# Values held stationary in attention's sums over keys, a later residual scale and two experts summed by products

## The chip, the cores and the metric

The kernel runs on one core of a Trainium2 chip. Its time is the device time of one execution, in microseconds (us). Before the change it is 2874.34 us, the median of three runs (2862.95 to 2874.93). The engines are TensorE (PE; its weight loads are listed apart as PEld), VectorE (DVE), ScalarE (ACT), GpSimd (POOL) and SyncE (SP, which issues most DMAs). Each has a queue of its own and works it off in order.

## The reference

Two blocks of layers follow each other on 512 rows of width 1024, all in fp32. What the change touches is this:

```
P = softmax(mask(q k^T * scale + bias)) ;  o = P v        # per head, 64 wide, 128 queries at a time
  forgetting attention: 8 heads, causal                   (first block, stage ab)
  dilated attention:    8 heads, causal; sliding window with a sink: 8 heads   (stage cd)
  nsa: 16 heads; o = g0*o_compressed + g1*o_selected + g2*o_window             (second block)

h   = layer_norm(alpha*h + mix, ln_mix_g, ln_mix_b)
gate= top-2 of 16 experts per row, by groups of 4
ffn = sum_e gate[:, e] * (silu(h Wg_e) * (h Wu_e)) Wd_e
h   = layer_norm(alpha*h + ffn, ln_ffn_g, ln_ffn_b)       # twice, with gdn and with nsa as mix
```

512 keys are all that a query can select, so the selected branch of nsa is causal attention too, and so is its window.

## The kernel before

The program is written with a tile framework: tiles come from pools with a fixed number of buffers (three for P, three for the turned P, three for either half of a weight piece, two PSUM banks `lin`, one `pt`, three `s`, two `o`), and a scheduler sets the order of the instructions on every engine. Matrices are multiplied as high and low parts in fp32r: a weight piece of 128x1024 is copied from `ws` to `wh` on ACT (L130), and `wl = ws - wh` is made on DVE (L131). One such linear product is three matmuls (L151 to L153). The stages follow each other: ab with the forgetting attention, a cross attention, an MLP, cd with the dilated and the sliding attention, cross attention, MLP, then gdn, expert layer 0 (`out_moe`), nsa, expert layer 1.

**Attention.** `probs` multiplies queries with keys into a PSUM tile `s` (L296), DVE adds the bias strip and takes the minimum `mn` (L301, L302), and ACT writes P = exp and its row sum `den` (L304). `pv` turns P block by block on PE (L312), copies it out of PSUM (L781 on ACT or L783 on DVE in turn), and multiplies it with the values, P stationary and 64 columns of values moving, in plain fp32 (L316), which the trace shows as two records per matmul. Eight heads and query blocks share a PSUM tile; `o_norm` divides by `den` (L323), or in nsa `gated` multiplies with the gate over `den` and adds up the three branches (L1749, L1751 on DVE, L1753 on POOL); `pair_out` turns the result back (L332). The attention of nsa runs in eight chunks of two heads, each with a compressed branch (L1680 to L1703) and two causal ones.

**Expert layer.** `out_moe` finishes the mixer's output product into z, takes mean and variance of z, and keeps z in high and low parts `Rh`, `Rl`. `rescale` (L1204, L1205) then makes z the residual for the second LayerNorm, z*G + B, on POOL. `moe` finds the mask M of the chosen experts (L1310, a chain of small DVE operations), counts places with M on PE (L1342 to L1346), and loads the largest count for a branch on all engines (L1379, L1380): its body handles overfull experts and isn't entered here. Then, two experts at a time, one-hot matrices `oh` (L1508, DVE) gather rows of R by products (L1519), the expert's three matrices are applied, and its rows `ey` go to a table `yd` in DRAM. Each row of z is to get two experts' rows: POOL gathers the first of them from `yd` in four indirect DMAs (L1441) after expert 13, and DVE adds them (L1435); the second after the last expert, added by L1241 in `ln_out`. Only expert 15 is left out of the table and added by products with `oh` turned (L1232, L1233). `ln_out` does the second LayerNorm: square on ACT (L1243), a root by small DVE operations (L231 to L241), centring on ACT (L1246), times `ln_ffn_g` on POOL for three of four tiles (L1247), and the last step on DVE (L1258). R is what the next stage turns first (L1266).

## Time and profile before

| what | us |
|---|---|
| median of three runs | 2874.34 |
| profiled execution, its own time | 2872.59 |
| span of that execution in the trace | 2870.8 |
| PE, DVE, ACT, POOL busy | 2684.3, 1783.8, 1368.9, 231.1 |
| forgetting, dilated, sliding, nsa attention (stretches) | 118 to 205, 815 to 888, 888 to 995, 2287 to 2526 |
| expert layer 0: routing, loop, end | 1895 to 1930, 1930 to 2155, 2155 to 2190 |
| expert layer 1: routing, loop, end | 2575 to 2605, 2605 to 2835, 2835 to 2871 |

A stretch is a window of the span with the work of one stage; neighbours overlap, since the scheduler starts the next projections early. Busy time of an engine in a stretch against its length tells how near that engine is to being the limit there; idle time of the others costs nothing by itself. A wait is put down to the instruction that released it last.

### The profile page before, as it was taken

To read this page: it belongs to the slowest core of one execution; us is meant where nothing else is said; L and a number is where in the kernel's file an instruction comes from. 1 tells how busy PE (TensorE), PEld (TensorE's weight loads), DVE (VectorE), ACT (ScalarE), POOL (GpSimd) and SP (SyncE) were. 2 spreads that over 40 slices of the span, in tenths; PEclk is the share of its full clock that TensorE was granted. 3 is DMA by queue.
4 is the path that set the end of the run, shared out by engine and by line. 5 is a ranking of instruction groups with operands and counts; after the bars stand their busy time and mean duration, and the time that the engine had idled before them with its cause. 6 is when DMAs were issued, how large, how long until landed. Compare 5 with 4: busy or idle time off the path is not lost. (4 is left out here: it accounts for less than half of the span.)

```text
span 2870.8 us, 40089 instructions
## 1 busy us (share of the span) xinstructions
PE 2684.3 (94%) x15088; PEld 2290.8 (80%) x15088; DVE 1783.8 (62%) x3539; ACT 1368.9 (48%) x2545; POOL 231.1 (8%) x207
## 2 busy tenths in 40 slices
PE   8999999999999999999999999969986999986994
PEld 6888888888888988888887888967865888885873
DVE  6675564444457556545347777677766477677667
ACT  5654442333356434332246444327763355525774
POOL 1101010000111010000010000020001011011001
PEclk9999999999999999999999999979998999997998
DMA  4314133333233322335323222327885202013786
GB/s 134 98 56 137 60 107 96 96 95 99 86 88 85 125 78 63 104 100 176 99 93 120 69 69 80 103 65 244 263 282 181 66 23 74 16 49 128 260 264 218
DMA packets 123112, 333.65 MB, mean 116 GB/s; under 512 B 21781, under 2 KB 37813, under 8 KB 122905
## 3 DMA queue, kind: packets, MB, share of 16 engines
q1 hardware_dynamic: 120472, 322.48, 35.8%
q0 software_dynamic: 2432, 8.46, 0.8%
q8 instruction: 124, 2.03, 0.3%
q14 instruction: 84, 0.68, 0.1%
HBM read 301.49 MB, written 29.07 MB: 115 GB/s over the span
## 5 line engine op out<-in xcount | busy, mean ns | idle before, releaser
L130 ACT ACTIVATE wh<-ws 128x1024 fp32r<-128x1024 f32 (+2 forms) x521 | 534.1, 1030 | 888.5 <-PE lin L152 609.5
L131 DVE TENSOR_TENSOR wl<-ws,wh 128x1024 fp32r<-128x1024 f32 (+2 forms) x521 | 622.1, 1199 | 230.8 <-ACT wh L130 228.7
L151 PE MATMUL lin<-xs,wh 128*128 128x512 f32 (+2 forms) x1080 | 427.3, 396 | 7.7 <-ACT xs L196 6.3
L152 PE MATMUL lin<-xs,wh 128*128 128x512 f32 (+2 forms) x1080 | 427.7, 396 | 2.6 <-DVE xs L197 2.6
L153 PE MATMUL lin<-xs,wl 128*128 128x512 f32 (+2 forms) x1080 | 426.5, 395 | 0.9 <-DVE wl L131 0.9
L151 PEld LDWEIGHTS lin<-xs,wh 128*128 128x128 f32 (+2 forms) x1080 | 202.1, 187 | 51.0 <-ACT xs L196 7.2
L152 PEld LDWEIGHTS lin<-xs,wh 128*128 128x128 f32 (+2 forms) x1080 | 202.2, 187 | 47.2 <-DVE xs L197 6.9
L153 PEld LDWEIGHTS lin<-xs,wl 128*128 128x128 f32 (+2 forms) x1080 | 202.1, 187 | 42.1 <-DVE wl L131 1.4
L346 DVE TENSOR_TENSOR h<-lin,h 128x512 f32<-128x512 f32 x112 | 77.4, 691 | 247.7 <-PE lin L153 247.6
L151 PE MATMUL lin<-sr,wh 128*128 128x512 f32 x512 | 199.2, 389 | 0.0
L152 PE MATMUL lin<-sr,wh 128*128 128x512 f32 x512 | 199.2, 389 | 0.0
L153 PE MATMUL lin<-sr,wl 128*128 128x512 f32 x512 | 199.2, 389 | 0.0
L733 DVE SCALAR_TENSOR_TENSOR ra<-lin,bc 128x512 f32<-128x512 f32 x64 | 44.3, 692 | 166.8 <-PE lin L153 164.3
L1519 PE MATMUL o<-oh,Rh 128*128 128x256 f32 x512 | 133.5, 293 | 8.1 <-PEq L1380 4.9
L304 ACT ACTIVATE P<-s,mn 128x256 f32<-128x256 f32 (+1 forms) x224 | 114.2, 514 | 52.4 <-DVE mn L302 50.0
L1519 PE MATMUL o<-oh,Rl 128*128 128x256 f32 x512 | 132.1, 290 | 3.7 <-PEq L1380 3.7
L152 PE MATMUL s<-wl,exh 128*128 128x512 f32 x256 | 106.2, 415 | 12.7 <-DVE wl L131 12.6
L151 PE MATMUL s<-wh,exh 128*128 128x512 f32 x256 | 102.9, 405 | 12.3 <-ACT wh L130 12.1
L153 PEld LDWEIGHTS lin<-sr,wl 128*128 128x128 f32 x512 | 96.1, 188 | 20.1
L152 PEld LDWEIGHTS lin<-sr,wh 128*128 128x128 f32 x512 | 96.1, 188 | 19.9
L151 PEld LDWEIGHTS lin<-sr,wh 128*128 128x128 f32 x512 | 96.1, 188 | 19.8
L1519 PEld LDWEIGHTS o<-oh,Rh 128*128 128x128 f32 x512 | 101.3, 198 | 12.1 <-DVE oh L1508 7.0
(605 smaller groups left out, 6225.0 us busy)
## 6 DMA issues: line engine op xcount, KB each, us to landing
ws<-in_moe_wgu SPq DMA_DIRECT2D x128, 512.0 KB, 5.3
ws<-in_mlp_wu SPq DMA_DIRECT2D x64, 512.0 KB, 3.6
ws<-in_mlp_wd SPq DMA_DIRECT2D x64, 512.0 KB, 3.6
ws<-in_moe_wd SPq DMA_DIRECT2D x64, 512.0 KB, 5.2
yd<-ey SPq DMA_DIRECT2D x60, 256.0 KB, 3.3
ws<-in_gdn_w SPq DMA_DIRECT2D x24, 512.0 KB, 3.6
ws<-in_ab_w SPq DMA_DIRECT2D x16, 512.0 KB, 4.3
ws<-in_xa_wk SPq DMA_DIRECT2D x16, 512.0 KB, 3.8
```

The lines of the kernel that those rows point to most:

```text
L130: nc.scalar.activation(wh, ws, AF.Copy)
L131: nc.vector.tensor_tensor(wl, ws, rd(wh), op=OP.subtract)
L151: mm(out, a[0], b[0], start=start, stop=False)
L152: mm(out, a[0], b[1], start=False, stop=False)
L153: mm(out, a[1], b[0], start=False, stop=stop)
L304: nc.scalar.activation(P[:, :nk], p[:, :nk], AF.Exp, bias=mn, scale=-1.0, accum_out=den)
L346: self.nc.vector.tensor_tensor(self.hT[n], p, self.hT[n], op=OP.add)
L733: nc.vector.scalar_tensor_tensor(a, p, 0.0, rms()[1], op0=OP.max, op1=OP.mult)
L1519: nc.tensor.matmul(p[:, j * 256:(j + 1) * 256], Rs[t][i][:, f * 128:(f + 1) * 128], oh[:, t], start=t + i == 0, stop=t == NT - 1 and i == 1)
```

## The change

It has three parts.

1. *Attention.* Each P is divided by its row sum before it is turned (`weigh`: a reciprocal of 128x1 on DVE, L335, then a multiplication of P on POOL, with the gate of the branch in nsa). `turn` turns P as before, three PSUM tiles per causal head, and splits them in high and low parts (ACT one, DVE the other, L107 and L108). The values are kept as one fp32r tile with high and low part side by side, 128 columns per head, and are the stationary operand; the turned P moves, 128 to 256 columns at a time, and sums for all 512 queries gather in one PSUM tile per head (`causal`, twelve matmuls; eight for a sliding head). `head_out` adds its two halves, and nothing is turned back. In nsa the compressed branch gathers into the same tile, and the next chunk's is computed ahead. Two of three turned tiles of a head take buffers of the weight pieces. The sink of the sliding attention becomes one more column of the exponential. For room, the residual of ab and cd is dropped and loaded again (16 DMAs, after 8 writes in cd), and nsa's bias strips are loaded per chunk and not ahead of expert layer 0.
2. *Residual scale.* z*G + B is done by DVE in the expert loop, one tile after experts 5, 7, 9 and 11; two of the four split pairs of z and the first one-hot products are written in other places around the branch.
3. *Last two experts.* Experts 14 and 15 are both left out of the table and added by products; both gathers from DRAM follow expert 13; `ln_out` does its centring and gain in one DVE operation per tile and no longer on ACT and POOL.

The core of the diff:

```diff
+    def weigh(self, P, nk, den, gate=None):
+        r = self.small((128, 1), "rd")
+        self.nc.vector.reciprocal(r, den)
+        if gate is None:
+            self.nc.gpsimd.tensor_scalar(P[:, :nk], P[:, :nk], r, None, op0=OP.mult)
+        else:
+            self.nc.gpsimd.tensor_scalar(P[:, :nk], P[:, :nk], r, gate, op0=OP.mult, op1=OP.mult)
+
+    def turn(self, Ps, PT):
+        p, n = self.psum("o"), 0
+        for P, nb in Ps:
+            for b in range(nb):
+                self.nc.tensor.transpose(p[:, n * 128:(n + 1) * 128], P[:, b * 128:(b + 1) * 128], self.ident)
+                n += 1
+        self.split(p[:, :n * 128], *(x[:, :n * 128] for x in PT))
+
+    def turned(self):
+        self.uid += 1
+        return [self.wp.tile([128, 1024], F32R, tag=tag, name=f"PT{tag}_{self.uid}", bufs=BUFS[tag]) for tag in ("wh", "wl")]
+
+    def causal(self, o, P, V, first=True, last=True):
+        mm = self.nc.tensor.matmul
+        PT = self.turned()
+        for qb in (3, 2):
+            self.turn([(P(qb), qb + 1)], [x[:, (qb - 2) * 512:(qb - 1) * 512] for x in PT])
+        for k, i in ((0, 0), (1, 0), (1, 1), (3, 0), (3, 1), (2, 0), (2, 1), (0, 1)):
+            x = PT[i].rearrange("p (q c) -> p q c", q=2)[:, k // 3:, k * 128:(k + 1) * 128]
+            mm(o[:, 256 + k // 3 * 128:], V(k), x, start=first and k + i == 0, stop=False)
+        PT = [self.t("PT", F32R, "PT") for _ in range(2)]
+        p1 = P(1)
+        self.turn([(P(0), 1), (p1, 2)], PT)
+        for k, i in ((0, 0), (1, 0), (1, 1), (0, 1)):
+            mm(o[:, k * 128:256], V(k), PT[i][:, k * 256:256 + k * 128], start=False, stop=last and (k, i) == (0, 1))
+
+    def head_out(self, e, o, y):
+        u = self.t("oh")[:64]
+        self.nc.scalar.activation(u, o[64:], AF.Copy)
+        self.nc.vector.tensor_tensor(y[e * 64:e * 64 + 64], o[:64], u, op=OP.add)
...
-        def rescale(t):
-            nc.gpsimd.tensor_tensor(z[t], z[t], G, op=OP.mult)
-            nc.gpsimd.tensor_tensor(z[t], z[t], Bv, op=OP.add)
...
+    def rescale(self, x, gain):
+        for g, op in zip(gain, (OP.mult, OP.add)):
+            self.nc.vector.tensor_tensor(x, x, g, op=op)
...
-        for t in range(NT):
-            rescale(t)
-        space = self.all_space()
+        oh = self.one_hot(0, pos3, iota, "h")
+        begun = [self.gather(Rs, oh, r) for r in range(2)]
+        space = self.all_space("h")
         mx = nc.values_load(mxi[0:1, 0:1], min_val=0, max_val=S)
         with self.tc.If(mx > CAP):
...
         for i in range(0, 16, 2):
             h = [self.expert_up(layer, i + j, xT) for j in range(2)]
+            if i == 14:
+                break
             self.expert_down(layer, i, h[0], yd)
...
+            if i in (4, 6, 8, 10):
+                self.rescale(z[i // 2 - 2], gain)
             if i == 12:
                 ys = [self.collect(yd[:1 + 12 * CAP], idx[0], t) for t in range(NT)]
+                yg = [self.collect(yd[:1 + 14 * CAP], idx[1], t) for t in range(NT)]
...
-        y = self.expert_down(layer, 15, h[1], None)
-        yg = [self.collect(yd[:1 + 15 * CAP], idx[1], t) for t in range(NT)]
+        y = [self.expert_down(layer, 14 + e, h[e], None) for e in range(2)]
...
         def add(t):
-            nc.vector.scalar_tensor_tensor(z[t], yg[t], w[:, t:t + 1], z[t], op0=OP.mult, op1=OP.add, accum_out=m)
...
+            for c in range(2):
+                p, cs = self.psum("s" if (2 * t + c) % 5 < 3 else "o"), slice(c * S, (c + 1) * S)
+                for e in range(2):
+                    for i in range(2):
+                        nc.tensor.matmul(p, ohT[e][:, t * 128:(t + 1) * 128], y[e][i][:, cs], start=e + i == 0, stop=e + i == 2)
+                nc.vector.scalar_tensor_tensor(z[t][:, cs], p, w[:, t:t + 1], z[t][:, cs], op0=OP.mult, op1=OP.add,
+                                               accum_out=m[:, c:c + 1])
...
-            if t < NT - 1:
-                nc.scalar.activation(Rs[t], z[t], AF.Identity, bias=m)
-                nc.gpsimd.tensor_tensor(Rs[t], Rs[t], G, op=OP.mult)
-            else:
-                nc.vector.scalar_tensor_tensor(Rs[t], z[t], m, G, op0=OP.add, op1=OP.mult)
+            nc.vector.scalar_tensor_tensor(Rs[t], z[t], m, G, op0=OP.add, op1=OP.mult)
```

The order of POOL's queue at the routing of layer 0, up to the branch; z are the residual tiles (the last two of four are shown), the memsets belong to the body of the branch. Before:

```order
L1204 TENSOR_TENSOR z_15839<-z_15839,ln_mix_g_16125 128x1024
L1205 TENSOR_TENSOR z_15839<-z_15839,ln_mix_b_16127 128x1024
L1204 TENSOR_TENSOR z_15840<-z_15840,ln_mix_g_16125 128x1024
L1205 TENSOR_TENSOR z_15840<-z_15840,ln_mix_b_16127 128x1024
L1452 MEMSET ov_16624 128x2
L1452 MEMSET ov_16625 128x2
L1379 TENSOR_LOAD mxi_16590
L1380 COMPARE_AND_BRANCH
```

Now:

```order
L1554 MEMSET ovw_17198 128x2
L1554 MEMSET ov_17196 128x2
L1554 MEMSET ov_17197 128x2
L1467 TENSOR_LOAD mxi_17131
L1468 COMPARE_AND_BRANCH
```

All eight operations on z have left the queue.

DVE's queue of layer 0 around the gather that follows expert 13: `wl` are weight splits, `exl` and `ehs` an expert's inputs, `yg` the gathered rows. Before:

```order
L131 TENSOR_TENSOR wl_20431<-ws_20429,wh_20430 128x1024
L1435 SCALAR_TENSOR_TENSOR z_15837<-yg_20393,wl_18408,z_15837 128x512 x2
L131 TENSOR_TENSOR wl_20443<-ws_20441,wh_20442 128x1024
L131 TENSOR_TENSOR wl_20455<-ws_20453,wh_20454 128x1024
L131 TENSOR_TENSOR wl_20472<-ws_20470,wh_20471 128x1024
L1435 SCALAR_TENSOR_TENSOR z_15838<-yg_20397,wl_18408,z_15838 128x512
L131 TENSOR_TENSOR wl_20484<-ws_20482,wh_20483 128x1024
L1537 SCALAR_TENSOR_TENSOR eh_20465<-eh_20465,s_20416 128x256
L1435 SCALAR_TENSOR_TENSOR z_15838<-yg_20397,wl_18408,z_15838 128x512
```

Now:

```order
L108 TENSOR_TENSOR exl_20854<-ex_20894,exh_20853 128x512
L131 TENSOR_TENSOR wl_21006<-ws_21004,wh_21005 128x1024
L1510 SCALAR_TENSOR_TENSOR z_16378<-yg_20937,wl_18943,z_16378 128x512 x2
L1510 SCALAR_TENSOR_TENSOR z_16379<-yg_20941,wl_18943,z_16379 128x512 x2
L1510 SCALAR_TENSOR_TENSOR z_16380<-yg_20945,wl_18943,z_16380 128x512 x2
L1510 SCALAR_TENSOR_TENSOR z_16381<-yg_20949,wl_18943,z_16381 128x512 x2
L131 TENSOR_TENSOR wl_21018<-ws_21016,wh_21017 128x1024
L131 TENSOR_TENSOR wl_21030<-ws_21028,wh_21029 128x1024
L131 TENSOR_TENSOR wl_21047<-ws_21045,wh_21046 128x1024
```

The additions of the first gather stood singly or in twos between weight splits, and now stand eight in a row ahead of the next three.

DVE's queue inside a chunk of nsa: L302 takes the minimum of a tile `s` (its second row reads the result `mn`), ACT's exponential needs it, and `den` is the sum that ACT writes. Before:

```order
L301 TENSOR_REDUCE mf_22374<-s_22370 128x1
L1751 TENSOR_TENSOR acc_22148<-pt_22174,rg_22295 128x512
L302 ISA s_22370,mn_22348<-s_22370,strip_18301,mf_22374 128x256
L302 ISA mn_22348 128x1
L783 COPY PT_22364<-o_22359 128x512
L301 TENSOR_REDUCE mf_22393<-s_22389 128x1
L1751 TENSOR_TENSOR gtmp_22345<-pt_22340,rc_22169 128x512
L302 ISA s_22389,mn_22348<-s_22389,strip_18300,mf_22393 128x256
L302 ISA mn_22348 128x1
L301 TENSOR_REDUCE mf_22410<-s_22406 128x1
```

Now:

```order
L301 TENSOR_REDUCE mf_23784<-s_23780 128x1
L108 TENSOR_TENSOR PT_23723<-o_23746,PT_23722 128x384
L302 ISA s_23780,mn_23778<-s_23780,strip_23012,mf_23784 128x256
L302 ISA mn_23778 128x1
L335 RECIPROCAL rd_23788<-den_23779 128x1
L302 ISA s_23809,mn_23807<-s_23809,strip_23012 128x256
L302 ISA mn_23807 128x1
L108 TENSOR_TENSOR PTwl_23757<-o_23771,PTwh_23756 128x512
L335 RECIPROCAL rd_23815<-den_23808 128x1
```

The reciprocal of each `den` follows the minimum of the same tile, after no instruction or one.

## Rows read from the trace of the kernel before

**Rows 1.** The page: the span, and TensorE's busy time, share of the span and instructions.
```profile
span 2870.8 us, 40089 instructions
...
PE 2684.3 (94%) x15088; PEld 2290.8 (80%) x15088; DVE 1783.8 (62%) x3539; ACT 1368.9 (48%) x2545; POOL 231.1 (8%) x207
```

**Rows 2.** The table of stretches: length, busy time of each engine, granted clock, DMA.
```profile
core 0: us, PE busy (x) PEld busy (x) DVE busy (x) ACT busy (x) POOL busy (x), PEclk, DMA share, GB/s
118.00:205.00 87.00, 81.77 (x534) 71.09 (x533) 67.61 (x186) 57.99 (x138) 8.76 (x11) 1.00 0.13 41
815.00:888.00 73.00, 72.30 (x434) 61.83 (x433) 53.09 (x117) 48.34 (x108) 16.80 (x16) 1.00 0.30 81
888.00:995.00 107.00, 103.24 (x756) 96.12 (x755) 74.38 (x177) 61.29 (x154) 5.10 (x4) 0.95 0.38 116
2287.00:2526.00 239.00, 230.56 (x1650) 208.06 (x1649) 171.79 (x580) 131.49 (x372) 25.37 (x46) 0.98 0.11 36
1930.00:2155.00 225.00, 207.74 (x1103) 172.31 (x1102) 159.71 (x204) 165.62 (x251) 5.49 (x5) 0.98 0.80 263
```

**Rows 3.** What PE waited for, whole span: us in total, times, longest.
```profile
PE pt L1342 <- DVE M L1310: 33.7, 2, 17.5
```

**Rows 4.** Timelines of DVE and POOL before M: start, duration, engine, operation [idle, releaser].
```profile
1893.00 2.30 DVE L241 SCALAR_TENSOR_TENSOR b<-u,b 128x1 f32<-128x1 f32 x1
...
1904.14 0.16 DVE L241 SCALAR_TENSOR_TENSOR b<-u,b 128x1 f32<-128x1 f32 x1
...
1916.99 2.34 POOL L1205 TENSOR_TENSOR z<-z,ln_mix_b 128x1024 f32<-128x1024 f32 x1
...
1917.13 2.28 DVE L1310 TENSOR_TENSOR M<-e1e,e2e 128x64 fp32r<-128x64 f32 x1
...
2598.15 2.36 DVE L1310 TENSOR_TENSOR e2e<-e2e,e1e 128x64 f32<-128x64 f32 x1
```

**Rows 5.** Timelines of DVE, POOL and PE behind the last expert of both layers.
```profile
2168.03 1.29 DVE L1241 SCALAR_TENSOR_TENSOR z<-yg,wh,z 128x1024 f32<-128x1024 f32 x1 [2.17 <-DMA yg<-yd,ii]
...
2173.07 8.92 POOL L1247 TENSOR_TENSOR R<-R,ln_ffn_g 128x1024 f32<-128x1024 f32 x3 [6.90 <-ACT R L1246]
...
2173.25 3.25 DVE L131 TENSOR_TENSOR wl<-ws,wh 128x1024 fp32r<-128x1024 f32 x1
...
2185.63 1.12 PE L1266 MATMUL o<-c_ident,R 128*128 128x128 f32 x4 [22.28 <-DVE R L1258]
...
2851.04 1.82 DVE L237 SCALAR_TENSOR_TENSOR u<-b,h 128x1 f32<-128x1 f32 x1
```

**Rows 6.** Groups by line, nsa attention: count, busy us, mean ns, idle before, releasers.
```profile
L316 PE MATMUL pt<-vv,PT 128*128 128x64 f32 x640 | 88.5, 280 | 2.9 <-ACT PT L781 1.3 <-DVE PT L783 0.4
...
L304 ACT ACTIVATE P<-s,mn 128x512 f32<-128x512 f32 (+3 forms) x128 | 66.7, 525 | 34.7 <-DVE mn L302 32.8 <-PE o L312 1.4
...
L783 DVE COPY PT<-o 128x512 f32<-128x512 f32 (+1 forms) x64 | 31.4, 490 | 38.8 <-PE o L312 36.8 <-PE s L296 1.2
...
L304 ACT ACTIVATION_READ_ACCUMULATOR P<-s,mn 128x1 f32 x128 | 25.2, 197 | 0.0
...
L1749 DVE SCALAR_TENSOR_TENSOR acc<-pt,rg,acc 128x64 f32<-128x64 f32 x64 | 13.0, 278 | 2.0 <-PE pt L316 1.8 <-POOL ovx L1452 0.2
...
L131 DVE TENSOR_TENSOR wl<-ws,wh 128x1024 fp32r<-128x1024 f32 x10 | 12.2, 1222 | 0.6 <-ACT wh L130 0.5
...
L1753 POOL TENSOR_TENSOR acc<-acc,gtmp 128x512 f32<-128x512 f32 x8 | 10.2, 1277 | 117.0 <-DVE gtmp L1751 117.0
```

**Rows 7.** Timeline of PE: PV records, and products of 256 columns.
```profile
889.16 1.77 PE L316 MATMUL pt<-v,PT 128*128 128x64 f32 x14
...
2451.74 0.29 PE L151 MATMUL lin<-wh,ny 128*128 128x256 f32 x1
...
2451.86 0.28 PE L152 MATMUL lin<-wl,ny 128*128 128x256 f32 x1
```

**Rows 8.** What DVE waited for in the nsa attention.
```profile
DVE rg L1719 <- ACT P L304: 5.2, 10, 0.6
```

348 lines of the change are left out of this document (192 added, 156 removed).

## The prediction

> **What bounds the kernel now.** I read the page first: TensorE (PE) is busy for 2684.3 us of the span of 2870.8 [rows 1]. So time can come back in two kinds of place: where PE's own work shrinks, and where PE stands still. The table of stretches [rows 2] tells them apart. In the three attention stages of the first block (118 to 205, 815 to 888, 888 to 995 us) and in the nsa attention (2287 to 2526) PE is busy for 94 to 99% of the time, and VectorE (DVE) comes second with 70 to 78%. The list of PE's waits gives the largest hole: the routing mask M, 33.7 us in two waits, one per expert layer [rows 3]. The next one is R, the rows after the last LayerNorm of layer 0, 22.28 us [rows 5]. The change touches all of these.
>
> **Routing: POOL's rescale taken out.** Before M runs a chain of small DVE operations. One takes 0.16 us (1904.14), but six of layer 0 took some 2.2 us each, the first at 1893.00, the last, M, at 1917.13 [rows 4]. Each of the six lies under a multiplication or addition of 128x1024 on GpSimd (POOL): the one at 1916.99 takes 2.34 us, and M, started 0.14 us later, ends 0.08 us after it. These are the rescale of z, eight operations per layer. The change does them on DVE later. Six excesses of 2.0 us are 12; the order of DVE's queue up to M stays as it was, so I count 11.5 us in layer 0, and 11 in layer 1, where also six were stretched (the last at 2598.15, 2.36 us). The order holds five of the 32 gather products ahead of the branch, worth about 1 us a layer. **Sum 24 us, 20 to 26.**
>
> **The end of an expert layer.** PE's wait for R ends at 2185.63 [rows 5]. Inside it lie the second gather from DRAM, for which DVE still stood 2.17 us at 2168.03; four additions of 1.29 us after it; three POOL multiplications by the gain, 8.92 us from 2173.07; and two weight splits that these stretched, the first to 3.25 us, where one takes 1.22 [rows 6]. Now the last two experts come by products, nothing is gathered here, and DVE makes R. For the first R there is left a quarter of the additions, a square on ScalarE (ACT), a root, and two DVE operations of 1.29: about 9 us against 27 from the last expert product. But sixteen extra products of 512 columns (twice the 0.12 of 256 columns [rows 7], 3.8 us) come partly ahead of it, and the other three R follow at DVE's pace. I take 13 us for layer 0 (10 to 16). In layer 1 what goes is the stretch of three operations under the same POOL step (the first at 2851.04, 1.82 us; some 6 in all): 6 us (4 to 8). **Sum 19 us, 14 to 24.**
>
> **What the expert loop pays.** Eight DVE operations of 128x1024 per layer, at 1.22 us as a weight split [rows 6], are 9.8 us in a stretch of 225 in which DVE is busy for 160 and PE for 208 [rows 2]. They stand in DVE's queue ahead of weight splits for which PE waits next; and the additions of the first gather, so far singly between splits, now stand eight in a row (four tiles at 1.29, 5.2 us) behind the landing of the gather. Their cover is the weight tiles split ahead. If it holds, nothing is lost; if it fails, 9.8 and 5.2 a layer. I take 2.5, nearer to the free end, since DVE has 65 us to spare. **Loss 5 us, 0 to 30.**
>
> **Attention, PE's part.** Fourteen PV records of 64 columns take 1.77 us [rows 7], of which the last one's 0.28 [rows 6] overlaps nothing: 0.115 from start to start. nsa has 640 [rows 6], 74 us, and loses 64 products and 48 transposes besides, 12 us. It gets 32 causal heads of twelve products with at most 256 columns, 0.12 each [rows 7], 1.4 us a head, and 7 us of others: 52. PE saves 33 us there, by the same count 9 in each of the first two stages of the first block, and 7 in the third. PE in nsa would be at 198 of the present 239 us.
>
> **Attention, DVE's part.** In nsa DVE loses 64 copies of the turned P (31.4 us), 64 additions of 128x64 (13.0) [rows 6] and some 16 of gating. It gets, per head, three splits of 1280 columns in all, which today's four copies of 0.49 show as 1.8 us, together 58; 16 additions of two halves of 512 columns, half of 1.29 each, 10; and 128 reciprocals at 0.1 to 0.19, 13 to 24. So its work goes from 172 to about 200 us, level with PE. And there is a new wait. The reciprocal needs the sum of the exponentials, which ACT writes with the same P. The order has 50 of nsa's 128 reciprocals directly behind the read of their own minimum, and 39 with one instruction between. ACT needs 0.525 us for the mean exponential and 0.197 to read its sum [rows 6], overlapping by some 0.1. DVE has this wait already, once a branch after the smallest P: 5.2 us in ten times [rows 8]. For larger P it is 0.6 to 0.8. Going through the order and taking off the work that stands between, I get some 40 us of waiting in nsa and 5 in each other stage. 200 and 40 are 240: **the DVE queue needs about what the stage takes now**, and PE's 33 us turn into waits on DVE. Part of the 40 may be time in which DVE would be idle anyway (67 us today). I take a gain of 3 us for nsa, between a gain of 28 (the waits fall into idle time) and a loss of 20 (they come on top). In the first block, with the same terms: forgetting attention, DVE 68, 14 and 5 are 87 of 87 us, no gain; dilated, 53, 14 and 5 are 72 of 73, 2 us; sliding, 74, 10 and 5 are 89 of 107 with PE at 96, 6 us. **Sum 11 us, from a loss of 25 to a gain of 48.**
>
> **POOL's new step.** Each P is multiplied on POOL before it is turned. No row shows POOL with one input; the nearest is its addition of 128x512, 1.277 us [rows 6]. I take that for the largest P as the upper end and half of it as the lower. At the upper, which I use, POOL works about 100 of nsa's 239 us, and a P comes 1.3 us later, with three buffers for P and 1.9 us per P. By itself that bounds nothing.
>
> M and the POOL row above it [rows 4] show a lock. The Trainium skill, page "SBUF — State Buffer", section "Who interferes with whom", says that a DVE instruction with two SBUF inputs contends with a GpSimd instruction that reads SBUF, and that the second to issue blocks fully. By this rule the new step, which reads P from SBUF, would bring into the attention what leaves the routing, and the second rival's sum would hold in place of mine.
>
> **The sum.** 24 and 19 less 5 is 38 us for the expert layers, and 11 for the attention: 49. The profiled execution took 2872.6 us (a span of 2870.8 and 1.8 around it), 1.7 under the median of 2874.3. 2872.6 less 49 is 2823.6: **2824 us.**
>
> **Rivals.**
> - The reciprocals' waits fall into idle time of DVE. For it: 36.8 us of DVE's idle time in nsa lie before the copies of P [rows 6], waiting for transposes. Then PE's saving shows, 28 in nsa and 20 in the first block; with 38 that is 86, 2787 us.
> - POOL's step holds DVE, as the rescale did. There are 224 P; it decides the sign once a P costs the path 0.23 us more than I count, for 52 us eat up 38 and 14 (the bound below). For it: the weight splits, the splits of Q and K in the forgetting attention, and the rotations of the dilated heads read two SBUF tiles. Against: most DVE steps of a P read PSUM and one tile. If every P stops DVE for half of a POOL step of 0.8 us, 224 times 0.4 are 90 us: **2914 us, slower than before**.
> - The expert loop takes back the routing's gain: DVE's block of additions and the rescales hold up the weight splits, 30 us in place of 5: 2849 us.
> - The routing doesn't shorten, because something else ends there last: 24 us less, 2848. The rows of M and POOL speak against it.
>
> **How the numbers follow.** Forecast 0.53, first rival 0.21, second 0.08, third and fourth together 0.18. A measurement of this kernel can tell about 0.5%, 14 us, from no change. The forecast's own spread is 2803 to 2847. The range goes down to the first rival with a few us under it, and up over the third: 2782 to 2862. Faster by over 0.5% (under 2860) holds the forecast, the first rival and most of the third: 0.85. Within 0.5%: the rest of the third, 0.07. Slower: the second, 0.08.
>
> **What the changed profile would show.** M's two waits at 8 to 9 us each, and no small DVE operation of 2 us ahead of them; R's wait at 8 to 12 us; reciprocals waiting for ACT's P for some 40 us in nsa, PE's busy time there near 198 and the stage still near 236 us. I am wrong if nsa shrinks by 20 us or more (the waits were covered), if DVE operations with two SBUF inputs take 2 us in numbers in the attention (the lock), or if PE's waits for wl in the expert loop grow by more than 10 us.

## The result and the profile after

The changed kernel takes **3059.07 us**, the median of four runs (3049.82 to 3065.92), against 2874.64 us before (four runs, 2862.95 to 2879.53): a ratio of 1.0642, with a 95% interval of 1.0613 to 1.0671. It is 184 us slower where 50 us of gain were forecast, and the time lies 197 us above the upper end of the range. It is also beyond the one rival that ended slower (2914).

The page after, whose two rows answer to [rows 1]:

```profile
span 3060.6 us, 39865 instructions
...
PE 2779.6 (91%) x14584; PEld 2320.9 (76%) x14584; DVE 1850.5 (60%) x3783; ACT 1436.1 (47%) x2677; POOL 368.8 (12%) x409
```

TensorE has 504 instructions less and is busy for 95 us more, while its share of the span falls from 94 to 91%. The table of stretches shows where; its rows stand for the forgetting, the dilated, the sliding and the nsa attention, each from the first to the last exponential (columns as in [rows 2]):

```profile
126.00:234.00 108.00, 81.50 (x363) 65.48 (x364) 69.20 (x200) 57.23 (x135) 43.29 (x41) 0.76 0.07 21
856.00:970.00 114.00, 85.45 (x370) 67.04 (x370) 67.56 (x167) 61.30 (x134) 52.90 (x45) 0.77 0.15 44
972.00:1105.00 133.00, 107.15 (x634) 92.76 (x633) 78.86 (x179) 69.74 (x171) 35.00 (x35) 0.82 0.34 105
2388.00:2709.00 321.00, 258.32 (x1262) 195.18 (x1262) 196.38 (x638) 163.04 (x424) 100.23 (x169) 0.86 0.10 30
```

The same stretches of before, cut in the same way, are 71, 75, 96 and 233 us long, with PE busy for 65.77, 74.75, 92.24 and 224.56. Now PE is busy for 75 to 81% of each, DVE for 59 to 64%, and the granted clock, 0.95 to 1.00 before, is 0.76 to 0.86. **All four stretches grew, and none has a full engine.** Of the 201 us that they grew in sum, 75 are busy time of PE, with 2629 records in place of 3198: at the lower clock the work that is left takes longer, as rows further down show for two kinds of product. What PE and DVE waited for, over the whole span (us in total, times, longest):

```profile
PE o L346 <- POOL P L337: 45.2, 41, 3.6
PE s L296 <- ACT P L308: 34.3, 57, 3.9
PE s L152 <- DVE wl L131: 18.8, 21, 6.8
PE o L1818 <- DVE Lp L108: 16.6, 8, 2.7
PE pt L1429 <- DVE M L1397: 16.4, 2, 8.4
...
PE o L346 <- POOL P L339: 11.0, 31, 1.3
...
PE o L1348 <- DVE R L1340: 9.4, 1, 9.4
```

```profile
DVE rd L335 <- ACT P L308: 61.2, 85, 1.2
DVE PTwl L108 <- ACT PTwh L107: 39.4, 48, 3.6
...
DVE PT L108 <- ACT PT L107: 29.1, 31, 2.1
```

The waits that the change was aimed at are cut: M from 33.7 [rows 3] to 16.4 in two, R from 22.28 [rows 5] to 9.4. In their place PE waits 56.2 us for POOL's multiplied P (L337 in the first block, L339 in nsa) and 34.3 before scores, until an exponential frees their PSUM tile. DVE stands 129.7 us behind ACT: 61.2 for the row sums that the reciprocals need (`rd`), 68.5 in the second half of each split.

Follow one P of 128x512 through the forgetting attention, after (timelines of ACT, DVE, POOL and PE: start, duration, engine, operation, then the idle time before it and its releaser):

```profile
138.49 0.69 ACT L308 ACTIVATE P<-s,mn 128x512 f32<-128x512 f32 x1 [1.33 <-DVE mn L302]
139.07 0.19 ACT L308 ACTIVATION_READ_ACCUMULATOR P<-s,mn 128x1 f32 x1
...
139.30 0.16 DVE L335 RECIPROCAL rd<-den 128x1 f32<-128x1 f32 x1 [0.93 <-ACT P L308]
...
139.63 1.56 POOL L337 TENSOR_SCALAR P<-P,rd 128x512 f32<-128x512 f32 x1 [1.40 <-PE s L296]
...
141.25 0.55 PE L346 MATMUL o<-c_ident,P 128*128 128x128 f32 x3 [0.81 <-POOL P L337]
...
142.69 0.60 ACT L107 ACTIVATE PTwh<-o 128x512 fp32r<-128x512 f32 x1
...
143.32 0.69 DVE L108 TENSOR_TENSOR PTwl<-o,PTwh 128x512 fp32r<-128x512 f32 x1
...
144.42 0.49 PE L365 MATMUL lin<-PTwh,v 128*128 128x256 f32 x2
```

And one of the same size before:

```profile
152.14 0.69 ACT L304 ACTIVATE P<-s,mn 128x512 f32<-128x512 f32 x1
...
152.97 0.66 PE L312 MATMUL o<-c_ident,P 128*128 128x128 f32 x4
...
153.66 0.60 ACT L781 ACTIVATE PT<-o 128x512 f32<-128x512 f32 x1 [0.75 <-PE o L312]
...
154.31 1.10 PE L316 MATMUL pt<-v,PT 128*128 128x64 f32 x8
```

From the exponential to the first product it was 2.17 us over two engines, and is 5.93 us over four; about 1 us of that goes to the second P of the group, whose split the first product also needs. Five hand-overs, six for the low half, stand where there were three, and between them PE, DVE and POOL wait in turn. Over all P of a stage, the mean time from the end of the exponential to the turn went from 0.8 to 3.1 us (forgetting), 0.8 to 4.9 (dilated) and 1.1 to 2.6 (nsa).

### The profile page after: what moved, and what is told of

Its sections match the earlier page's. It is cut to its first block, busy times and chain, and to the rows that moved or that the text cites. A ratio compares the mean times of both kernels' runs of the same rounds, so it can differ in the third digit from the quotient of the medians.

```text
span 3060.6 us, 39865 instructions
## 1 busy us (share of the span) xinstructions
PE 2779.6 (91%) x14584; PEld 2320.9 (76%) x14584; DVE 1850.5 (60%) x3783; ACT 1436.1 (47%) x2677; POOL 368.8 (12%) x409
## 5 line engine op out<-in xcount | busy, mean ns | idle before, releaser
L346 PE MATMUL o<-c_ident,P 128*128 128x128 f32 x536 | 115.3, 335 | 58.6 <-POOL P L337 45.2
L308 ACT ACTIVATE P<-s,mn 128x512 f32<-128x512 f32 (+1 forms) x224 | 115.4, 515 | 92.5 <-DVE mn L302 87.6
L346 PEld LDWEIGHTS o<-c_ident,P 128*128 128x128 f32 x536 | 75.2, 168 | 90.5 <-POOL P L337 57.2
L337 POOL TENSOR_SCALAR P<-P,rd 128x256 f32<-128x256 f32 (+2 forms) x96 | 110.6, 1154 | 210.1 <-DVE rd L335 178.6
L296 PE MATMUL s<-K,Q 128*128 128x512 f32 (+1 forms) x224 | 98.6, 443 | 40.1 <-ACT P L308 34.3
L152 PE MATMUL s<-wl,exh 128*128 128x512 f32 x256 | 109.2, 427 | 19.0 <-DVE wl L131 18.8
```

What stands on the lines that cost most here:

```text
L152: mm(out, a[0], b[1], start=False, stop=False)
L296: nc.tensor.matmul(p[:, :nk], q, k, start=i == 0, stop=i == len(qk) - 1)
L308: nc.scalar.activation(P[:, :n], p[:, :n], AF.Exp, bias=mn, scale=-1.0, accum_out=den)
L337: self.nc.gpsimd.tensor_scalar(P[:, :nk], P[:, :nk], r, None, op0=OP.mult)
L346: self.nc.tensor.transpose(p[:, n * 128:(n + 1) * 128], P[:, b * 128:(b + 1) * 128], self.ident)
```

## The experiments

Several of them leave out the division of P by its row sum. The gates of the expert layers are then others, experts become overfull, and the body of the branch runs, which adds some 1430 us; so only the three attention stages are compared in those. Before, after, e1, e12 and e18 were timed several times, the others once. The lengths of the stages, from the traces (first block: from the start of the kernel to the first residual addition; then the stage of dilated and sliding heads between two residual additions; then nsa's exponentials from the first to the last):

| run | forgetting stage | dilated and sliding | nsa | sum | time |
|---|---|---|---|---|---|
| before | 250.9 | 241.6 | 232.7 | 725.2 | 2874.6 |
| after | 288.5 | 321.0 | 322.1 | 931.6 | 3059.1 |
| e1 experts alone | 249.9 | 239.4 | 229.5 | 718.8 | 2852.4 |
| e2 no reciprocal | 280.7 | 308.7 | 299.1 | 888.5 | – |
| e3 no multiplication | 270.1 | 304.8 | 296.6 | 871.5 | – |
| e4 neither | 266.7 | 285.6 | 275.1 | 827.4 | – |
| e5 filler | 289.2 | 323.6 | 344.7 | 957.5 | 3074.8 |
| e6 two factors | 279.2 | 312.4 | 319.0 | 910.6 | 3034.7 |
| e7 high half | 297.0 | 321.4 | 308.2 | 926.6 | 3046.1 |
| e8 old products, divided | 274.4 | 259.5 | 304.4 | 838.3 | 2980.6 |
| e9 on VectorE | 283.8 | 306.9 | 338.5 | 929.2 | 3049.5 |
| e10 four P | 282.2 | 311.8 | 322.9 | 916.9 | 3037.8 |
| e11 heads interleaved | 283.8 | 325.6 | 321.5 | 930.9 | 3050.0 |
| e12 experts, additions spread | 248.8 | 241.6 | 229.6 | 720.0 | 2847.2 |
| e13 neither, high half | 256.3 | 276.9 | 247.6 | 780.8 | – |
| e14 the same, by P | 261.9 | 268.4 | 265.4 | 795.7 | – |
| e15 neither, by P | 277.5 | 294.0 | 339.4 | 910.9 | – |
| e16 divided, by P | 289.2 | 312.8 | 362.0 | 964.0 | 3085.9 |
| e17 neither, spread | 257.7 | 279.5 | 291.4 | 828.6 | – |
| e18 divided, spread | 271.5 | 300.2 | 333.1 | 904.8 | 3022.8 |

The stages lost 206.4 us, more than the whole kernel (184). The expert layers gained the rest. e1 and e12 have the attention of before, and their sums lie 6.4 and 5.2 us under it: by so much a sum differs without a cause in the attention.

**e1: the expert layers alone.** Before's attention with parts two and three of the change; the diff is against the changed kernel, at the forgetting attention.

```diff
-                    self.weigh(x, nk, den)
-                self.causal(o, P, lambda b: v[b][:, h * 128:(h + 1) * 128])
-                self.head_out(e, o, y)
+                self.pv(o[:, j * 64:(j + 1) * 64], P, nk, [v[b][:, h * 64:(h + 1) * 64] for b in range(qb + 1)])
+            self.pair_out(self.o_norm(o, den, 8), ys[4 + i])
```

> The kernel before with the second and third part of the change only (residual scale on DVE in the expert loop, experts 14 and 15 added by products); its attention is that of before. From the two traces, by the places of M, of the first R and of the end: layer 0 gains 10 us at the routing and 2 between M and R, layer 1 some 8 at the routing and loses 3 behind it. Theory 'the attention alone lost the time': 2855 to 2862 us. Rival 'the expert layers have a share in the loss, hidden by the shift of the stages': 2880 us or more.

2852.35 us, a ratio of 0.9933 (0.9912 to 0.9954): these two parts are worth some 19 us (13 to 25 by the interval), and the attention holds all of the loss. M's waits are 16.0 us in sum and R's 9.4. From the last down product to R the time went from 27.5 to 15.8 us in layer 0, and to DVE's last step on R from 29.1 to 22.0 in layer 1. But the loop, from the seventh gather product with `Rh` to the last down product, takes 238.2 and 241.4 us where it took 227.7 and 229.2. The timeline of DVE after expert 13 and the list of PE's waits, both of this run, show a part of the reason:

```profile
2128.59 1.23 DVE L131 TENSOR_TENSOR wl<-ws,wh 128x1024 fp32r<-128x1024 f32 x1 [2.67 <-ACT wh L130]
2129.73 5.38 DVE L1420 SCALAR_TENSOR_TENSOR z<-yg,wl,z 128x512 f32<-128x512 f32 x8
2135.03 3.49 DVE L131 TENSOR_TENSOR wl<-ws,wh 128x1024 fp32r<-128x1024 f32 x3
```

```profile
PE s L152 <- DVE wl L131: 18.6, 21, 7.4
```

Eight additions stand in one block of 5.38 us ahead of three weight splits, and PE's longest wait for `wl` is 7.4 us.

**e12: the same, with the block of additions broken up.**

```diff
-                for t in range(NT):
-                    add(ys, wts[0], t)
...
+        for t in range(NT):
+            add(ys, wts[0], t)
```

> The kernel of e1 (experts' part alone, 2852 us) with the additions of the first gathered rows written behind the last two experts' first halves instead of right after the gather, so that in DVE's queue they stand singly between weight splits. In e1 the last pair of experts took 63 us where it took 55 before, with a block of eight additions of 5.4 us in DVE's queue, and PE waiting up to 7 us for wl. If that block is the cause: 6 us come back per layer, 2840 us. If the 16 us more of work on DVE is the cause wherever it stands: 2850 us or more.

2847.24 us in six runs, a ratio of 0.9928 (0.9908 to 0.9949). The additions now come one to three at a time, and PE's waits for `wl` are 10.6 us in all, at most 0.8. The loop, measured as in e1, takes 234.0 and 236.4 us: the block was worth 4 to 5 us a layer in it, and some 13 of the 23 us that the loop lost stay. Behind the last down product of layer 0, R comes after 19.1 us in place of 15.8, so that most of the gain is lost again: from M to R, the layer takes 264.4 us (266.0 in e1, 265.9 before). The kernel beats before and after; from e1 the times can't tell it apart, and the answer lies between the two theories.

**e2, e3, e4: the division taken apart.** e2 leaves out the reciprocal (P is multiplied by one), e3 the multiplication (second diff), e4 both.

```diff
-        r = self.small((128, 1), "rd")
-        self.nc.vector.reciprocal(r, den)
+        r = self.ones[:, 0:1]
```

```diff
-        if gate is None:
-            self.nc.gpsimd.tensor_scalar(P[:, :nk], P[:, :nk], r, None, op0=OP.mult)
-        else:
-            self.nc.gpsimd.tensor_scalar(P[:, :nk], P[:, :nk], r, gate, op0=OP.mult, op1=OP.mult)
```

> The changed kernel without the reciprocals: POOL multiplies each P by a constant 1 (and the gate in nsa), so the division by the row sum is left out. Theory R (DVE stands at the reciprocal until ACT has the row sum, and its queue is held; this is what the prediction priced at 40 us in nsa): half of the 205 us or more come back, 2960 us or less. Theory L (the multiplication on POOL lengthens the way from ACT to PE, 1.1 us in the mean in the first block and 0.65 in nsa, and hand-overs around it): little comes back, 3010 us or more.

> The changed kernel without POOL's multiplication: the reciprocals stay on DVE, nothing reads them, P goes to PE as ACT wrote it (division and gates are left out). Theory R: DVE still stands at each reciprocal, 3000 us or more. Theory L: PE no longer waits for POOL, 2930 us or less.

> The changed kernel with neither the reciprocals nor the multiplication (division and gates are left out). If the two together are the cause: the attention falls to its old length or under it, since PE has 58 us less work, 2800 to 2870 us. If the cause lies behind them (the split of the turned P on ACT and then DVE, the one PSUM tile per head, the weight pieces' buffers): 2950 us or more.

The reciprocal is worth 43 us, the multiplication 60, both together 104: they add up, as steps one behind the other do. Taken off the 3059 us of after, these are 3016, 2999 and 2955 us: the reciprocal gave back little, the multiplication an amount between its two theories, and e4 says that half of the cause lies behind both. PE's wait for POOL is 56.2 us, near the 60 that leaving the step out gives, but the wait doesn't vanish with it. PE then waits for the same tiles straight from ACT (lists of PE's waits: one row of before, of e3 and of e4):

```profile
PE o L312 <- ACT P L304: 11.4, 10, 3.1
PE o L342 <- ACT P L308: 60.0, 50, 3.9
PE o L341 <- ACT P L308: 41.1, 37, 3.9
```

102 us of the 206 stay without any division.

**e6: the multiplication with a second factor of one.** In nsa, where it multiplies by `rd` and by the gate, it is the shorter one (groups by form, after):

```profile
L337 POOL TENSOR_SCALAR P<-P,rd 128x512 f32<-128x512 f32 x16 | 25.6, 1597 | 30.9 <-DVE rd L335 24.3 <-DVE u L240 3.8 <-PE s L296 1.4
L339 POOL TENSOR_SCALAR P<-P,rd,gt 128x512 f32<-128x512 f32 x32 | 24.6, 770 | 51.4 <-DVE rd L335 45.3 <-PE pt L370 2.3 <-DVE mf L301 2.2
```

```diff
-            self.nc.gpsimd.tensor_scalar(P[:, :nk], P[:, :nk], r, None, op0=OP.mult)
...
+        self.nc.gpsimd.tensor_scalar(P[:, :nk], P[:, :nk], r, 1.0 if gate is None else gate, op0=OP.mult, op1=OP.mult)
```

> The changed kernel with a second factor 1.0 in POOL's multiplication in the first block, as nsa's has one (its gate). In the trace the multiplication of 128x512 takes 1.60 us with one factor and 0.77 with two. If that is the form and not what runs beside it, the first block's multiplications fall to about half, and the 96 of them get 50 us shorter in all. Theory L (POOL's latency stands in the way of PE): the first block loses 25 us or more of its 117, 3035 us or less. Theory R (the reciprocal): under 10 us.

3034.74 us. The step now takes less than half (groups by form, this run):

```profile
L336 POOL TENSOR_SCALAR P<-P,rd 128x512 f32<-128x512 f32 x16 | 11.1, 692 | 31.5 <-DVE rd L335 27.0 <-DVE u L240 2.2 <-PE o L343 1.4
```

Sixteen times 0.905 us and the smaller forms, some 47 us of POOL's time, give 18 us in the first two columns of the table, where 25 were the bound: a shorter step helps, as far as nothing else comes last.

**e9: the multiplication on VectorE.** There it takes 507 ns for 128x512 with the constant one, 537 with a gate, and needs no hand-over to POOL.

```diff
-            self.nc.gpsimd.tensor_scalar(P[:, :nk], P[:, :nk], r, None, op0=OP.mult)
...
+        self.nc.vector.tensor_scalar(P[:, :nk], P[:, :nk], r, 1.0 if gate is None else gate, op0=OP.mult, op1=OP.mult)
```

> The changed kernel with the multiplication of P on DVE in place of POOL, right behind the reciprocal (a second factor 1.0 in the first block, the gate in nsa). No hand-over to POOL and back, no port of POOL's, but 224 operations more on DVE. Theory L (the way from ACT over DVE and POOL to PE is what PE waits for): the three stages, 932 us with the change, get 50 us shorter or more, about 3000 us. Theory R (DVE's queue is what holds it): longer still, 3060 us or more.

3049.47 us, just under the fastest of after's four runs, and between the two theories. The first block gains 18.8 us, much as with e6, nsa loses 16.4: there DVE has more work already, and what a P saves on the way its queue pays.

**e8: before's products with the division on the way.** Before's attention, P stationary and 64 columns of values moving; only forgetting, dilated and nsa heads divide each P on POOL instead of the sums.

```diff
+        if divide:
+            r = self.small((128, 1), "rd")
+            nc.vector.reciprocal(r, den)
+            if divide == 2:
+                nc.gpsimd.tensor_scalar(P[:, :nk], P[:, :nk], r, 1.0, op0=OP.mult, op1=OP.mult)
+            else:
+                nc.gpsimd.tensor_scalar(P[:, :nk], P[:, :nk], r, None, op0=OP.mult)
```

> The kernel before with its own products, but each P of the forgetting, the dilated and the nsa attention is divided on the way as in the change (reciprocal on DVE, multiplication on POOL; in nsa with a second factor 1.0), and the division behind is dropped. 192 P. If the division alone is what costs, whatever PE does: half of the loss of the changed kernel or more, 2960 us or more. If it costs since PE has less work to put into the waits: its PV products cover most of it, 2880 to 2920 us.

2980.59 us, 106 over before. The stages are 113 longer (in nsa a part of it is linear products that the order pulled in: 394 in place of 244), and the sliding heads, which don't divide, take what they took, 94.0 us against 94.6. So the division in this place costs over 100 us by itself, also with before's form of the products.

**e5: more work for PE.** Six products of the identity in each turn, to keep the clock up.

```diff
+        for _ in range(6):
+            self.nc.tensor.transpose(p[:, :128], self.ident, self.ident)
```

> The changed kernel, and ahead of the transposes of each turn six transposes of the identity into the same PSUM tile, which nothing reads: 160 turns x 6 x 0.109 = 105 us more work for PE, and nothing else. Theory C (a large part of the loss is TensorE's clock, which stood at 0.76 to 0.86 in the attention stages, since PE stands still so often): the fillers lie in PE's waits, the granted clock rises over 0.93 in these stages, and the kernel is no slower than the changed one, perhaps 20 to 60 us faster. Rival (the waits alone, the clock only follows): the added work shows in part, 30 to 100 us slower.

```profile
126.00:234.00 108.00, 85.70 (x504) 72.16 (x505) 71.50 (x206) 60.12 (x139) 43.93 (x42) 0.91 0.07 23
```

This row is the stretch of the forgetting attention: the granted clock is 0.91 in place of 0.76, and in nsa 0.95 in place of 0.86. The time is 3074.79 us, 16 over after: neither a gain nor the 30 us of the rival. The stage from the start to the first residual addition stays (289.2 against 288.5), nsa grows by 22.6. So the low clock follows from PE's waiting, since it rises when the waits are filled. That it costs nothing isn't shown: of the 105 us that the fillers add by the estimate, most don't appear in the time, which the higher clock and the waits that they fill can both explain.

**e10, e11: more P at a time.** e10 is e6 with four buffers for P, and one less for common temporary tiles. e11 is e6 with the two heads of a pair in turn.

```diff
-BUFS = {"t": 6, "x": 16, "h": 4, "y": 10, "P": 3, "PT": 3, "bc": 2, "ws": 4, "wh": 3, "wl": 3}
+BUFS = {"t": 5, "x": 16, "h": 4, "y": 10, "P": 4, "PT": 3, "bc": 2, "ws": 4, "wh": 3, "wl": 3}
```

```diff
-                self.causal(o, P, lambda b: v[b][:, h * 128:(h + 1) * 128])
-                self.head_out(e, o, y)
+            for _ in zip(head(0), head(1)):
+                pass
+            for e in range(2):
+                self.head_out(e, os[e], y)
```

> The kernel of e6 (two factors; 3035 us) with four buffers for P in place of three, and five in place of six for the common temporary tiles to make room. Theory B (each P is held longer, from ACT until PE has turned it, so three buffers leave too few in flight): 20 us faster or more, 3015 us or less. Rival (the order fixes who waits for whom, whatever the buffers): within 10 us of 3035.

> The kernel of e6 (3035 us) with the two heads of a pair step by step in turn in the forgetting and the dilated attention, as their query blocks stood before the change; nsa and the sliding attention stay. Theory H (the change works off one head after the other, four P of one chain, where before two heads stood side by side): the stages ab and cd, 279 and 312 us in e6, get 25 us shorter together or more. Rival: under 10 us.

3037.82 and 3050.0 us against 3034.74 of e6: neither brings a gain, and the two stages that e11 changes are 18 us longer with it.

**e7 and e13: the low half left out.** Of the turned P only the high half is kept (one copy on ACT or DVE in turn, half of the products): e7 with the division, e13 without.

```diff
-        self.split(p[:, :n * 128], *(x[:, :n * 128] for x in PT))
+        self.copy(PT[0][:, :n * 128], p[:, :n * 128])
...
-        for k, i in ((0, 0), (1, 0), (1, 1), (3, 0), (3, 1), (2, 0), (2, 1), (0, 1)):
+        for k, i in ((0, 0), (1, 0), (3, 0), (2, 0)):
```

> The changed kernel without the low half of the turned P: one copy to fp32r per turn, by ACT and DVE in turn, in place of ACT's copy and DVE's difference after it; the products with the low half and with the low half's share are left out (5 of 12 per causal head, 4 of 8 per sliding head stay out), so P has less precision. Theory S (the split in series is the other half of the loss, since the kernel without division still needed 827 us in the three stages that took 725): the three stages get 60 us shorter or more, 3000 us or less. Rival (the chain from the products with the keys to ACT and back holds it): 20 us or less.

> Leaves out the division by the row sums and, of the turned P, the low half with its split and its products; the turned P is copied once (ScalarE or VectorE in turn), as before the change. Without a right gate the overfull branch runs, so only the three attention stages compare (to the first residual add, the dilated and sliding stage, the nsa exponentials: 725 us in sum before, 932 after, 827 without the division alone). If the split in two steps one after the other is what costs the remaining 102 us, the sum falls to 700 to 750, since PE also loses half of its products. If it is the form in which products wait for two turned P and P stand in a queue of three, the sum stays above 800, as when the low half alone was left out (15 us of gain).

With the division it gives 5 us in the three stages (14 in nsa, and a loss in the first block), no more than a sum differs by itself; without the division it gives 47, from 827.4 to 780.8. That lies between what the two theories gave. So the low half, its step in the split together with its products, is a good part of the 102 us, but only once the division no longer comes last; and 56 us over before are left with half of the products with the values gone. nsa in e13 (stretch of its exponentials):

```profile
3778.00:4027.00 249.00, 205.08 (x1082) 160.36 (x1083) 156.77 (x465) 139.64 (x380) 19.17 (x43) 0.88 0.12 38
```

PE does two thirds of the instructions of before (1082 for 1607), and the stretch is 16 us longer.

**e14, e15, e16: products for each P by itself.** No product waits for a second P; a causal head has products of 128 columns behind each turn (10 of the high half, 20 of both). e14 is e13 with this, e15 is e4, e16 is e6.

```diff
+        for qb in (3, 2, 1, 0):
...
+            self.turn([(P(qb), qb + 1)], x)
+            for i in range(2):
+                for k in range(qb + 1):
+                    mm(o[:, qb * 128:qb * 128 + 128], V(k), x[i][:, k * 128:k * 128 + 128],
...
```

> As the run with neither division nor low half, but in the causal heads each P is turned by itself and its products (128 columns each, 10 per head in place of 6) follow at once, so that no product waits for a second P. If the grouping of two P is the cause, the sum of the three stages falls by 30 us or more against that run; if not, it stays within 10 us or rises by the four products more (some 0.3 us a head, 15 us in all).

> No division, both halves of the turned P, and products that follow each P by itself in the causal heads. Against 827 us of the run without division: the grouping as cause would give 790 or less; the split in series as cause would leave 815 to 845.

> The whole computation, with the multiplication in the form with two factors (3035 us, 911 us in the three stages) and products that follow each P by itself. If the grouping costs, 2980 to 3015 us; if the way of a P through four engines is what counts, 3025 to 3060.

e14 rises by 15 us, as much as was said of the added products, though in its parts it doesn't follow them (nsa 18 up, the dilated stage 8 down). e15 rises by 83 and e16 to 3085.93 us, past what any of the theories gave. The grouping is no cause: taken away, it makes things worse. Why most with the low half isn't shown: PE's waits for the halves of the turned P are 25.5 us in e15 and 23.2 in e4.

**e17, e18: linear products between the P.** In the changed order PE's linear products for the next pair stand in long rows of their own: in e4, 24 of 32 P of the forgetting attention have none between their scores and their turn (8 before), and 23 of 32 dilated (3 before). Here they are written between the P; e17 is e4 with this, e18 is e6.

```diff
-            self.lin_f(w, (4 + i, 8 + i), xs, ev)
+            self.lin_later(w, (4 + i, 8 + i), xs, ev)
...
         for qb in (3, 2):
-            self.turn([(P(qb), qb + 1)], [x[:, (qb - 2) * 512:(qb - 1) * 512] for x in PT])
+            x = P(qb)
+            self.fill(self.nfill)
+            self.turn([(x, qb + 1)], [x[:, (qb - 2) * 512:(qb - 1) * 512] for x in PT])
```

> Leaves out the division (so only the three attention stages compare). The linear products of the next pair, which in the changed kernel stand in long rows of their own, are written between the P: before each turn and ahead of the products of a head. In the order, 8 of 32 P of the forgetting attention have no linear product between their scores and their turn (24 of 32 in the run with neither, 8 before the change), 5 of 32 in the dilated (23; 3 before), 86 of 128 in nsa (99; 36 before). If the missing cover is what remains of the loss without the division, the exponentials of the forgetting attention span 69 to 76 us (85.9 without the spreading), the dilated ones 74 to 84 (98.7), and nsa loses some 10 us of 275. If the cover doesn't matter, all three stay within 4 us.

> The whole computation, with the multiplication in its form with two factors (3035 us; spans of the exponentials 95.9, 106.5, 130.5, 319.0 us) and the same spreading. If cover for the way of a P through ScalarE, VectorE and GpSimd is what the changed order lacks, forgetting and dilated attention fall by 12 to 25 us each and nsa by some 10: 2980 to 3010 us, still slower than before the change. If the way itself sets the pace, whatever stands between, the time stays at 3025 to 3045.

A part of it came. Without the division the forgetting stage gains 9.0 us and the stage of the dilated heads 6.1 (their exponentials span 85.6 us in place of 98.7, where 74 to 84 were forecast), but nsa loses 16.3, so the sum stays at 828.6. With the division, 3022.79 us (3016.63 to 3027.38), a ratio to before of 1.0522 (1.0496 to 1.0547): 12 us better than e6, nearer to what the rival gave. The missing cover costs some 15 us in the first block, not the rest; why nsa loses by the spreading isn't shown.

## Why the prediction was wrong

**Routing: right mechanism, a little too large.** Said were 24 us, M's waits at 8 to 9 us. They are 8.0 and 8.4, and the small operations ahead of M are no longer stretched (DVE's timeline, after: the operation on M of layer 0 that took 2.28 us in [rows 4], and the same one of layer 1, which took 2.37):

```profile
2026.68 0.22 DVE L1397 TENSOR_TENSOR M<-e1e,e2e 128x64 fp32r<-128x64 f32 x1
...
2784.44 0.22 DVE L1397 TENSOR_TENSOR M<-e1e,e2e 128x64 fp32r<-128x64 f32 x1
```

In e1, from the last residual addition to M the time fell by 7.3 us in layer 0, and from nsa's last exponential to M by 12.1 in layer 1: 19, just under the lower bound of 20.

**The ends: right.** 19 were said (13 and 6); e1 shows 11.7 and 7.1.

**The loop: right mechanism, wrong size.** A loss of 5 us was said, with 30 as the end of the range; e1 shows 10.5 and 12.2, 23 us. I took the weight tiles split ahead as cover and valued the block of eight additions near the free end. The row of 5.38 us and the wait of 7.4 put it on the path, and e12, which breaks it up, shortens the loop by 4.2 and 5.0. The rest has no run of its own. By the last down product of each expert, e1 keeps the pace of before within 2 us up to expert 13, so the four rescales, which the trace has before expert 3's last down product, cost nothing that shows; the whole loss falls to the last two experts, where the eight additions of the second gather now stand too. My sum put those at nothing in the loop.

**Attention: the step that failed.** "By itself that bounds nothing" was said of POOL's step, and the whole part went by loads: the work of each engine plus its waits, and the largest of these as the length of the stage. Many terms of it came out. The reciprocals wait 61.2 us in all, at most 1.2 at a time (55 said, from [rows 8]; 41.8 in nsa, for 40), DVE is busy for 196.4 us in nsa (200), POOL for 100 (100). What did not hold is the inference. **A stage in which every engine has time to spare can still grow, when each P has a longer way and only a few P are on the way.** I had put the longer way at nothing, and its steps showed: 43 us for the reciprocal, 60 for the multiplication, and 47 for the low half with the division gone. DVE's queue is the plainest case: while a reciprocal or a low half waits for ACT, the minimum of the next P stands behind it, and so its exponential, and PE's next scores wait for that exponential's PSUM tile (34.3 us; 0.4 before, 27.5 in e2). ACT's waits for that minimum, before, after and without the reciprocals (lists of ACT's waits; the last row is of e2):

```profile
ACT P L304 <- DVE mn L302: 50.0, 79, 1.8
ACT P L308 <- DVE mn L302: 87.6, 81, 2.2
ACT P L308 <- DVE mn L302: 41.4, 40, 2.4
```

My 40 us of waits in nsa were put on DVE alone, and were to end in its idle time or beside PE's saving; these rows show them handed on to ACT and PE.

PE's saving itself didn't appear. nsa was to need 198 us of PE, and shows 258.3, at a clock of 0.86 in place of 0.98; without the division (e4), at 0.90, 231.4. Products that the change left as they were take longer, the turns of P (L312, now L346) and the scores (groups by form of PE in the stretch of nsa, two rows of before, two of after):

```profile
L312 PE MATMUL o<-c_ident,P 128*128 128x128 f32 x316 | 56.4, 282 | 5.3 <-ACT P L304 5.3
L296 PE MATMUL s<-K,Q 128*128 128x512 f32 x30 | 13.5, 450 | 0.0
...
L346 PE MATMUL o<-c_ident,P 128*128 128x128 f32 x317 | 64.1, 321 | 13.4 <-POOL P L339 11.0 <-POOL Lc L1801 1.9
L296 PE MATMUL s<-K,Q 128*128 128x512 f32 x31 | 18.6, 600 | 7.6 <-ACT P L308 7.6
```

A turn takes 321 ns in place of 282, 1.14 times as much, which is the ratio of the two clocks; in e4 it is 307. By that ratio the 258.3 us would be 227 at the old clock, an estimate: about half of the 60 us too many go with the clock, which I had left where it was. The scores of 512 columns grew by more than that, 600 in place of 450 ns; why, no run tells. Nor does one tell whether the new products cost more than the 0.12 us of a place without pauses.

POOL's price was also outside its bounds in the first block: 1.597 us for 128x512, where 1.277 was the upper end; in nsa 0.770 lay within. As e6 shows, this is some 24 of the 184 us.

**The rivals.** The third came near in its term: the loop paid 23 us where it said 30. The second had the right sign, by another mechanism. It said that POOL's step stops DVE operations with two SBUF inputs, at half a step for every P. Such operations in the forgetting attention after (groups by form of DVE):

```profile
L131 DVE TENSOR_TENSOR wl<-ws,wh 128x1024 fp32r<-128x1024 f32 x6 | 7.5, 1252 | 0.8 <-ACT wh L130 0.7
...
L280 DVE TENSOR_TENSOR KL<-qk,K 64x512 fp32r<-64x512 f32 x5 | 3.4, 687 | 1.6 <-ACT K L279 1.5
...
L588 DVE TENSOR_TENSOR g<-uc,g 128x512 f32<-128x512 f32 x3 | 2.7, 903 | 0.0
```

Before, these took 1236, 684 and 672 ns in the mean: only the last is longer, 0.7 us in three. The Trainium skill, page "SBUF — State Buffer", section "Who interferes with whom", has such operations contend with a GpSimd instruction that reads SBUF. By the same section of the Trainium skill, an operation with at most one SBUF input doesn't contend, outside DVE's modes that use two ports. The trace agrees: the second step of a split of 128x512 in the four stretches, which reads PSUM and one SBUF tile, takes 689 ns in the mean where it lies under a POOL step for three tenths of its time or more (11 of them) and 690 where not (45). Of 43 weight splits, which read two SBUF tiles, 13 lay under one, and took 1245 ns in the mean and at most 1428, in place of 1224. So DVE's operations were hardly held, and the lock isn't the price; e9, without POOL in the attention, gains only 10 us. But the rival's point of decision was right: a P needed to cost the path only 0.23 us more, and 206 us over 224 P are 0.92.

**What stays open.** Of the 102 us that the new form costs without any division, 47 are the low half, with its split and its products, and some 15, in the first block, the missing linear products between the P. These two were each measured with the other in place, so they may overlap. For the remaining 40 no run gives a cause. The grouping is excluded, and so are the buffers for P and the sequence of heads, these two only with the division in place. The lists of waits say where PE stands: in e4 for exponentials, 41.1 us ahead of the turns (11.4 before) and 16.3 ahead of the scores (0.4 before). Three parts of the new form were not tried alone: turned tiles in buffers of the weight pieces, one PSUM tile per head, and the residual loaded again. For two of them the trace of after shows no price: PE waits 3.0 us for weight pieces in the four stretches, and no engine for the residual loaded again. How much of the loss goes through the clock is open as well.

## What to carry to other kernels

Where an inner loop runs round several engines with in-order queues and few tiles on the way, price a change by the hand-overs that it adds to one tile's way, times the number of tiles, before any engine's load is summed. A division moved from the sums to each P belongs there: on 224 P it cost over 100 us in this kernel, 0.46 us for each, where the idle time of every engine had promised a price near nothing. And a block of off-path work in a queue that feeds PE can come in nearly full on the path, as the eight additions did; where it is moved to, it may cost again.

## What was not expected of the hardware

GpSimd's multiplication of 128x512 by one factor per partition took 1597 ns, with a second factor, be it a gate or the constant one, 770 and 692; at 128x128 it is 760 against 481 and 504. The clock granted to TensorE was 0.76 to 0.86 of full speed in the four stretches, a mean between its levels of 1.2 and 2.4 GHz, while PE stood waiting for 19 to 25% of them; six idle products per turn brought it to 0.91 in the first of them without any gain in time.
